# First layer of a two-layer decoder step: where in the input projection the attention's score, transpose and value work stands

## The chip, the core and the metric

The kernel runs on one core of one Trainium2 chip. The metric is the device time of one execution in microseconds. Three runs of the kernel before took 590.7, 591.06 and 591.3 us; the median is 591.06.

Engines are named as in the profile: PE is TensorE (PEld its weight loads), DVE is VectorE, ACT is ScalarE, POOL is GpSimd, SP is the engine that issues most DMAs.

## What is computed

One inference step of two layers over 256 prompt rows (one sequence) and 8 sample rows (each with 256 past positions in paged caches), all with shared weights. The change lies in layer 0, whose mixer is

```python
def moba_gmlp_mixer(x, pos, past_kv, norm_g, w_in, sgu_gain, sgu_w, sgu_b, w_out):
    h = rmsnorm(x, norm_g)
    q, k, v, bu, bv = jnp.split(h @ w_in, ...)
    q, k = rope_partial(q, pos), rope_partial(k, pos)
    a = moba_attention(q, k_all, v_all, pos)          # softmax attention, 8 heads of 64
    bvn = layer_norm(jax.nn.gelu(bv), sgu_gain)
    b_out = spatial_gating(jax.nn.gelu(bu), bvn, sgu_w, sgu_b)   # u * (w @ v + b), chunks of 128
    return x + jnp.concatenate([a, b_out], axis=-1) @ w_out
```

With 256 prompt positions and a block of 256, the prompt's attention is plain causal softmax, and a sample's attention runs over its 256 past positions and its own. After the mixer come a convolution FFN, the second layer (other mixers) and a last norm; the change does not touch them.

## The kernel before

**Projections.** Activations stand transposed (128 partitions by 264 = 256 + 8 columns). Each weight block of 128 x 128 is multiplied in three fp32r matmuls (high x high, low x high, high x low; `mm` in the profile), so one block is 3 mm. Eight blocks make a weight tile: ACT writes its high half (`wh`, L304), DVE the low half (`wl`, L305), into four rotating buffers, three tiles ahead of PE. `run` (L311) goes through the blocks of a phase and calls hooks at given block numbers. Phase `in0` (the input projection of layer 0) has 160 blocks in the order bv, q, k, bu, v; phase `out0` (the output projection) follows and starts with the operand catB.

**Hooks.** `blk(b, f)` places the instructions of `f` behind block b. PE's order is the order in which the program is written (`fixed`, L210); the order of the other engines is set by a scheduler when the kernel is built. It is the same in every execution.

**The work between the blocks.** `s_qk(t)` (L776) multiplies the scores S of one tile of two heads (S_6 and S_7 are those of tile 3) in plain fp32; `s_soft` (L785) takes their maxima with DVE into p (two passes over each S, each followed by a small read of the accumulator into st), exponentiates on ACT and normalizes. `s_tr(t)` (L797) transposes p on PE (`pt`) and copies it to SBUF (`pT`), by ACT for tiles 0 and 1, by DVE for 2 and 3. `sm_score` (L931) multiplies the samples' scores `sc` with the cached keys (32 matmuls and 4 small ones, one PSUM bank); `sm_soft` (L811) is their softmax, `sm_tr` (L830) the transposes. `sample_av` (L519) multiplies them with the cached values (`pv_l`), `sm_out` (L843) transposes that (`po_l`). `v_turn` (L560) transposes the value tiles (`vtp_v`), `s_av` (L801) multiplies the values (`pav`) into catA. `gm_gate` (L910) makes the gate's products `pf`, and DVE and ACT make catB of them. `gm_var` and `gm_norm` are the layer norm of bv (`mu`, `sq`, `bsq`, `ns_sgu`).

**PSUM.** Eight banks: four (`psm`, tag mm) for the projections and some helpers, four (`psa`, tag at, L233) for S, pt, sc, pv_l, po_l, vtp_v and pav. A bank is handed on when its readers are done; the program makes the first matmul of the next owner wait for them.

**Buffers.** A pool of 24 (`up`) holds key and value tiles, p's transposes and other 4 KB tiles by turns.

Of the kernel before, what the change touches and what calls it, by code (L numbers as in the profile page):

```python
# [13 lines left out]
AF = mybir.ActivationFunctionType  # L14
# [192 lines left out]
def tile_decoder_step(ctx: ExitStack, tc: tile.TileContext, a):  # L207
    nc = tc.nc
    v, s, g = nc.vector, nc.scalar, nc.gpsimd
# [25 lines left out]
    def f4(name, shape=(P, 4, T), dt=F32):  # L235
        return up.tile(list(shape), dt, tag="u", name=name)
# [7 lines left out]
    def at(name):  # L244
        return psa.tile([P, 512], F32, tag="at", name=name)
# [217 lines left out]
    def behind(i, j):  # L463

        tc.add_manual_dep(i.ins, j.ins.name, mybir.DependencyInfo(mybir.DependencyClass.NoSync, mybir.DependencyReason.DATA), reason="order")
# [7 lines left out]
    def page_list(cache, name):  # L473

        tiles, todo = [], []

        def load(i):
            if i >= len(regs):
                page_regs(1)
            if i % NPG == 0:  # L480
                tiles.append(f4(f"{name}_{i}", (P, NPG, 512)))
            late(tiles[i // NPG][:, i % NPG, :], cache[bass.ds(regs[i], 1), :, :].rearrange("o p f -> (o p) f"))

        return tiles, [lambda i=i: load(i) for i in range(NS * NPG)]
# [34 lines left out]
    def sample_av(st, pz, vtiles, name):  # L519
        pv = at(f"pv_{name}")  # L520
        for gr in range(2):
            for pg in range(NPG):
                for j in range(4):
                    sq = 4 * gr + j
                    pe.matmul(pv[32 * j:32 * j + 32, :], pz[:, pg, sq, :], vtiles[sq][:, pg, :],
                              start=gr + pg == 0, stop=gr + pg == NPG, skip_group_check=True)
        s.activation(st["msk"], pv, AF.Copy)
# [17 lines left out]
    PZ = con.tile([P, NPG, NS, 32], F32, name="PZ")  # L545
# [5 lines left out]
    def turn(blocks, name, bank=None):  # L551

        ps = [(bank or at)(f"{name}_{r}") for r in range(2)]
        for i, x in enumerate(blocks):
            for r, p in enumerate(ps):
                a0 = r * HF
                pe.transpose(p[:, i * HF:(i + 1) * HF], x[a0:a0 + HF, :], ident[a0:a0 + HF, a0:a0 + HF])
        return ps

    def v_turn(vt, src, ts, name, bank=None, e=None):  # L560
        n = len(ts)
        ps = turn([src[:, t, kb * P:(kb + 1) * P] for kb in range(2) for t in ts], f"vtp_{name}{ts[0]}", bank)
        for r, p in enumerate(ps):
            d, x = vt.rearrange("p b (t r d) -> p b t r d", r=2, d=HF)[:, :, ts[0]:ts[0] + n, r, :], p[:, :2 * n * HF].rearrange("p (b t d) -> p b t d", b=2, t=n)
            v.tensor_copy(d, x) if (e[r] if isinstance(e, tuple) else e) is v else s.activation(d, x, AF.Copy)

    def p_turn(dst, ws, name, pin=False, e=None):
        ps = turn([w[:, i * P:(i + 1) * P] for w in ws for i in range(3)], name)
        for r, p in enumerate(ps):
            d, x = dst.rearrange("p h (i r d) -> p (h i) r d", r=2, d=HF)[:, :, r, :], p[:, :6 * HF].rearrange("p (x d) -> p x d", d=HF)  # L570
            i = v.tensor_copy(d, x) if e is v else s.activation(d, x, AF.Copy)
            if pin:
                tc.keep_in_program_order(i)

    def av(pav, vt, w, h):
        o = pav[64 * (h % 2):64 * (h % 2) + 64, :SEQ]
        pe.matmul(o, vt[:, 0, h * HD:(h + 1) * HD], w[:, :SEQ], start=True, stop=False)
        pe.matmul(o[:, P:], vt[:, 1, h * HD:(h + 1) * HD], w[:, SEQ:], start=False, stop=True)
# [79 lines left out]
    def pick(xg):  # L658
        return lambda m, k: hl(xg, k)
# [107 lines left out]
    vtiles, vload = page_list(a["vp0"], "V0")  # L767
    st0 = {}
# [7 lines left out]
    def s_qk(t):  # L776
        pss, hd = [at(f"S0_{2 * t + i}") for i in range(2)], heads(t)
        for ps, (qh, kh) in zip(pss, hd):
            tc.keep_in_program_order(pe.matmul(ps[:, 0:P], qh[:, 0:P], kh[:, 0:P], start=True, stop=False, skip_group_check=True))
        for ps, (qh, kh) in zip(pss, hd):  # L780
            tc.keep_in_program_order(pe.matmul(ps[:, P:384], qh[:, P:SEQ], kh[:, 0:SEQ], start=False, stop=True, skip_group_check=True))
        for i, ps in enumerate(pss):
            s_soft(2 * t + i, ps)

    def s_soft(h, ps):  # L785
        st = sm.tile([P, 4], F32, tag="st", name=f"st0_{h}")
        pr = pp.tile([P, 384], F32, tag="p", name=f"p0_{h}")
        for i, c in enumerate((slice(0, P), slice(P, 384))):
            v.tensor_tensor_reduce(out=pr[:, c], in0=ps[:, c], in1=maskb0[:, c], scale=-1.0, scalar=-NEG, op0=ALU.add, op1=ALU.min, accum_out=st[:, i:i + 1])
        for i, c in enumerate((slice(0, P), slice(P, 384))):  # L790
            s.activation(pr[:, c], pr[:, c], AF.Exp, bias=st[:, i:i + 1], scale=-1.0, accum_out=st[:, 2 + i:3 + i])
        v.reciprocal(st[:, 2:4], st[:, 2:4])
        v.tensor_scalar(pr[:, 0:P], pr[:, 0:P], st[:, 2:3], None, ALU.mult)
        s.activation(pr[:, P:384], pr[:, P:384], AF.Copy, scale=st[:, 3:4])
        st0["p", h] = pr

    def s_tr(t):  # L797
        pT = st0["pT", t] = f4(f"pT0_{t}", (P, 2, 384))
        p_turn(pT, [st0.pop(("p", 2 * t + i)) for i in range(2)], f"pt0_{t}", e=v if t > 1 else s)

    def s_av(t):  # L801
        w = st0.pop(("pT", t))
# [124 lines left out]
    blk = lambda b, f, *x: hk.at(b / 8 - 1, f, *x)  # L927
# [16 lines left out]
    blk(40, masks)  # L944
    blk(44, gm_first)
    blk(72, sm_q)
    for t, b in enumerate((96, 96, 112, 125)):
        blk(b, s_qk, t)
    for t, b in enumerate((112, 125)):
        blk(b, s_tr, t)  # L950
    blk(96, sgu_load)
    blk(132, sgu_mask)
    blk(90, gm_mean)
    blk(114, gm_var)
    blk(131, sm_score)
    blk(131, sm_soft)
    blk(132, gm_norm)
    blk(140, sm_tr)
    blk(141, gm_gelu)
    blk(143, lambda: nc.sync.dma_start(a["k0"], k4))  # L960
    blk(144, gm_tr)
    blk(144, s_tr, 2)
    blk(144, s_tr, 3)
    blk(152, gm_own)
    for t in range(4):
        blk(152, gm_gate, t)
    blk(159, lambda: sample_av(st0, PZ, vtiles, "l0"))
    run(orders["in0"], pick(xg), in0_evac, hk)
    nc.sync.dma_start(a["v0"], v4)
    hk = Hooks()  # L970
    blk(4, sm_out)
    blk(4, lambda: v_turn(vt, v4, range(4), "v0", e=(s, v)))
    for t in range(4):
        blk(9, s_av, t)
    blk(24, lnexp)
# [13 lines left out]
    vtiles, vload = page_list(a["vp1"], "V1")  # L989
# [64 lines left out]
    def z_tr(t, pin=False):  # L1054
        pT = st1["pT", t] = f4(f"pT1_{t}", (P, 2, 384))
        p_turn(pT, [st1.pop(("w", 2 * t + hh)) for hh in range(2)], f"pt1_{t}", pin)
# [72 lines left out]
    blk = lambda b, f, *x: hk.at(b / 8 - 1, f, *x)  # L1129
# [147 lines left out]
```

## Time and profile before

| | |
|---|---|
| median of 3 runs | 591.06 us |
| the profiled execution: its own time | 591.49 us |
| the profiled execution: its span, first to last instruction | 589.7 us |
| PE busy | 582.5 us, 99% |
| DVE busy | 429.0 us, 73% |
| ACT busy | 338.4 us, 57% |

The profile is of one execution. A timeline row gives start, length, engine, line, operation, output <- input and shape; rows of PE overlap, since matmuls are pipelined and their ends are modelled, so the distance between two starts tells more than a length. "[0.26 <-X]" is idle time of that engine ahead of the row and what ended it.

### The profile page before, as it was taken

The numbers are of one execution on the slowest core, as the hardware profiler recorded it, in microseconds if no ns is written. First come the engines' busy times: TensorE is split into PE (matmuls) and PEld (weight loads), VectorE is DVE, ScalarE is ACT, GpSimd is POOL, SyncE is SP. The second block draws the span as 40 slices with busy tenths as digits, with TensorE's granted clock in tenths as the row PEclk, the third lists the DMA queues.
The fourth block names the chain that finished last, engine by engine and source line by source line (L and its number), as shares of the span: only waits on it lengthen the run. The fifth ranks groups of instructions, "written<-read, shape, count | busy, mean of one in ns | idle before, by whom it ended". The sixth has DMA issues, their size and how long they took to land.

```text
span 589.7 us, 12427 instructions
## 1 busy us (share of the span) xinstructions
PE 582.5 (99%) x4972; PEld 566.3 (96%) x4972; DVE 429.0 (73%) x771; ACT 338.4 (57%) x597; POOL 45.2 (8%) x62
## 2 busy tenths in 40 slices
PE   9999999999999999999999999999999999999995
PEld 7999879999999999999999879999999999999995
DVE  6999876787877877566669675778787777756552
ACT  7849746665655655544454556567565565555431
POOL 1000213200000000011030000120000000002111
PEclk9999999999999999999999999999999999999998
DMA  8899764554545455894557762554554546464501
GB/s 331 327 399 368 265 224 166 189 203 159 211 152 206 161 198 177 298 361 172 197 210 287 262 217 89 180 204 169 189 186 172 202 157 215 150 216 158 201 1 73
DMA packets 27564, 122.42 MB, mean 208 GB/s; under 512 B 3314, under 2 KB 4466, under 8 KB 16114
## 3 DMA queue, kind: packets, MB, share of 16 engines
q1 hardware_dynamic: 27218, 121.28, 57.2%
q8 instruction: 39, 0.64, 0.4%
q10 hardware_dynamic: 288, 0.34, 0.2%
q14 instruction: 19, 0.16, 0.1%
HBM read 117.65 MB, written 3.96 MB: 206 GB/s over the span
## 4 chain that ended last, share of the span: by engine, by line
PE 95%; DMA 1%; DVE 1%; ACT 1%; issue 1%; SPq 0%; POOLq 0%
PE mm L219 89%; PE sc L219 1%; PE pv_l L219 1%; DMA xw<-in_xw 1%; PE pav L219 1%; PE Z L219 1%; PE S L219 1%; PE pt L222 1%; DVE wl L688 0%; PE pf L219 0%; PE pm L219 0%; ACT sqw L670 0%; SPq L370 0%; DVE xg_l L403 0%; DVE sqw L718 0%
## 5 line engine op out<-in xcount | busy, mean ns | idle before, releaser
L304 ACT ACTIVATE wh<-raw 128x1024 fp32r<-128x1024 f32 x177 | 187.4, 1061 | 196.9 <-PE mm L219 183.7
L305 DVE TENSOR_TENSOR wl<-raw,wh 128x1024 fp32r<-128x1024 f32 x177 | 217.4, 1229 | 104.8 <-ACT wh L304 104.2
L219 PE MATMUL mm<-xg_f_h,wh 128*128 128x264 f32 x704 | 199.9, 284 | 0.0
L219 PE MATMUL mm<-xg_f_h,wl 128*128 128x264 f32 x704 | 199.8, 284 | 0.0
L219 PE MATMUL mm<-xg_f_l,wh 128*128 128x264 f32 x704 | 198.6, 282 | 0.0
L219 PEld LDWEIGHTS mm<-xg_f_l,wh 128*128 128x128 f32 x704 | 132.8, 189 | 0.0
L219 PEld LDWEIGHTS mm<-xg_f_h,wh 128*128 128x128 f32 x704 | 132.5, 188 | 0.0
L219 PEld LDWEIGHTS mm<-xg_f_h,wl 128*128 128x128 f32 x704 | 132.4, 188 | 0.0
L219 PE MATMUL mm<-a_h,wl 128*128 128x264 f32 x352 | 100.0, 284 | 0.0
L219 PE MATMUL mm<-a_h,wh 128*128 128x264 f32 x352 | 100.0, 284 | 0.0
L219 PE MATMUL mm<-a_l,wh 128*128 128x264 f32 x352 | 99.7, 284 | 0.0
L219 PEld LDWEIGHTS mm<-a_l,wh 128*128 128x128 f32 x352 | 66.4, 189 | 0.0
L219 PEld LDWEIGHTS mm<-a_h,wh 128*128 128x128 f32 x352 | 66.2, 188 | 0.0
L219 PEld LDWEIGHTS mm<-a_h,wl 128*128 128x128 f32 x352 | 66.2, 188 | 0.0
L219 PE MATMUL mm<-xg_h,wh 128*128 128x264 f32 x160 | 44.4, 293 | 0.2 <-ACT xg_h L402 0.2
L219 PE MATMUL mm<-xg_h,wl 128*128 128x264 f32 x160 | 43.3, 285 | 0.1
L219 PE MATMUL mm<-xg_l,wh 128*128 128x264 f32 x160 | 43.0, 284 | 0.0
L219 PE MATMUL mm<-xg_n_h,wh 128*128 128x264 f32 x128 | 38.0, 297 | 0.0
L219 PE MATMUL mm<-xg_n_h,wl 128*128 128x264 f32 x128 | 36.4, 285 | 0.0
L219 PE MATMUL mm<-xg_n_l,wh 128*128 128x264 f32 x128 | 36.3, 284 | 0.0
L219 PEld LDWEIGHTS mm<-xg_h,wh 128*128 128x128 f32 x160 | 29.2, 189 | 2.3 <-issue 1.2
L219 PEld LDWEIGHTS mm<-xg_h,wl 128*128 128x128 f32 x160 | 29.2, 188 | 0.3 <-DVE wl L688 0.3
(260 smaller groups left out, 842.4 us busy)
## 6 DMA issues: line engine op xcount, KB each, us to landing
raw<-in_w SPq DMA_DIRECT2D x89, 1024.0 KB, 4.8
K<-in_kt SPq DMA_DIRECT2D x32, 256.0 KB, 7.4
V<-in_vp SPq DMA_DIRECT2D x32, 256.0 KB, 5.9
raw<-in_w SPq DMA_DIRECT2D x4, 512.0 KB, 8.7
X<-in_x SPq DMA_DIRECT2D x4, 264.0 KB, 4.6
xw<-in_xw SPq DMA_DIRECT2D x2, 388.0 KB, 4.9
out_y<-yo SPq DMA_DIRECT2D x2, 300.0 KB, 2.3
out_k<-k SPq DMA_DIRECT2D x1, 528.0 KB, 8.9
```

The costliest lines, as they stand in the source:

```text
L219: return self.keep(nc.tensor.matmul(*x, **k))
L222: return self.keep(nc.tensor.transpose(*x, **k))
L304: s.activation(h, src, AF.Copy)
L305: v.tensor_tensor(l, src, h.bitcast(F32), ALU.subtract)
```

## The change

Three hooks of phase `in0` move. The transposes of tile 1 go from block 125 to 128, and the scores of tile 3, which stood ahead of them, from 125 to 128, behind them. The samples' scores and their softmax go from 131 to 128, so that the three stand together. The gate's products go from block 152 to 150. The samples' values go from block 159 of `in0` to block 4 of `out0`, behind the value tiles' transposes, and `sm_out` from block 4 to 9, ahead of `s_av`. Beside that, the copies of pt 2 and 3 go from DVE to ACT, and the exponentials of heads 6 and 7 are ordered behind the last copy of p's transposes on ACT.

```diff
@@ p_turn
             if pin:
                 tc.keep_in_program_order(i)
+        return i
@@ s_soft
-            s.activation(pr[:, c], pr[:, c], AF.Exp, bias=st[:, i:i + 1], scale=-1.0, accum_out=st[:, 2 + i:3 + i])
+            e = s.activation(pr[:, c], pr[:, c], AF.Exp, bias=st[:, i:i + 1], scale=-1.0, accum_out=st[:, 2 + i:3 + i])
+            if h > 5:
+                behind(e, st0["turned"])
@@ s_tr
-        p_turn(pT, [st0.pop(("p", 2 * t + i)) for i in range(2)], f"pt0_{t}", e=v if t > 1 else s)
+        st0["turned"] = p_turn(pT, [st0.pop(("p", 2 * t + i)) for i in range(2)], f"pt0_{t}", e=s)
@@ the hooks of in0 and out0
...
+    blk(128, s_tr, 1)
+    blk(128, s_qk, 3)
...
+    blk(128, sm_score)
+    blk(128, sm_soft)
...
```

On PE, at the samples' scores, the order before was (K are the key tiles, qz the samples' queries; DMAHW, DVE and Activation are the semaphores that an instruction waits for):

```order
L219 MATMUL mm_1104<-xg_h,wh_896 128x264
L219 MATMUL mm_1104<-xg_l,wh_896 128x264
L219 MATMUL mm_1104<-xg_h,wl_897 128x264
L219 MATMUL sc_1114<-K_0_337,qz_l_144 32x256 [waits DMAHW1_49,DMAHW0_49,DVE_49]
L219 MATMUL sc_1114<-K_0_337,qz_l_144 32x256 x3
L219 MATMUL sc_1114<-K_2_406,qz_l_144 32x256 [waits DMAHW4_49,DMAHW3_49]
```

and on the same engine and place it is now:

```order
L222 MATMUL pt_1_1_1061<-CST,p_3_848 128x64
L219 MATMUL S_6_1076<-k_218,q_217 128x128
L219 MATMUL S_7_1077<-k_218,q_217 128x128 [waits Activation_49]
L219 MATMUL S_6_1076<-k_218,q_217 128x256
L219 MATMUL S_7_1077<-k_218,q_217 128x256
L219 MATMUL sc_1100<-K_0_337,qz_l_144 32x256 [waits DMAHW1_49,DMAHW0_49,DVE_49]
L219 MATMUL sc_1100<-K_0_337,qz_l_144 32x256 x3
L219 MATMUL sc_1100<-K_2_406,qz_l_144 32x256 [waits DMAHW4_49,DMAHW3_49]
```

Between S of tile 3 and sc there stood the transposes of tile 1 and 18 mm; now nothing stands there, and sc still waits for a count of DVE.

On DVE, at the passes over S of tile 3, the order before was:

```order
L887 TENSOR_TENSOR bv_220<-bv_220,mu 128x1056
L305 TENSOR_TENSOR wl_1023<-raw_761,wh_1022 128x1024
L789 ISA p_6_1052,st_6_1051<-S_6_1045,maskb_215 128x128
L789 ISA st_6_1051 128x1
L789 ISA p_6_1052,st_6_1051<-S_6_1045,maskb_215 128x256
L789 ISA st_6_1051 128x1
```

and on the same engine and place it is now (wl_1150 is the low half of weight tile 19, bu and bsq belong to the gate's branch):

```order
L890 TENSOR_TENSOR bv_220<-bv_220,mu 128x1056
L305 TENSOR_TENSOR wl_1023<-raw_761,wh_1022 128x1024
L765 TENSOR_TENSOR bu_221<-mm_1026,R_n_373 128x264
L869 TENSOR_TENSOR bsq<-sq_987 128x264
L870 TENSOR_TENSOR bsq<-bsq,sq_987 128x264
L305 TENSOR_TENSOR wl_1150<-raw_761,wh_1149 128x1024
L863 TENSOR_SCALAR tril<-CST 128x128
L871 TENSOR_TENSOR bsq<-bsq,sq_987 128x264
L790 ISA p_6_1083,st_6_1082<-S_6_1076,maskb_215 128x128
L790 ISA st_6_1082 128x1
L790 ISA p_6_1083,st_6_1082<-S_6_1076,maskb_215 128x256
L790 ISA st_6_1082 128x1
```

Six instructions now stand on DVE ahead of the passes over S_6, which before came straight behind the low half of tile 18.

## Rows read from the trace of the kernel before

**Rows 1.** The page: busy PE (us, share, instructions), and the last chain by engine.

```profile
PE 582.5 (99%) x4972; PEld 566.3 (96%) x4972; DVE 429.0 (73%) x771; ACT 338.4 (57%) x597; POOL 45.2 (8%) x62
...
PE 95%; DMA 1%; DVE 1%; ACT 1%; issue 1%; SPq 0%; POOLq 0%
```

**Rows 2.** Waits of PE: us in total, times, longest.

```profile
PE mm L219 <- ACT xg_h L402: 0.2, 1, 0.2
```

**Rows 3.** Timeline of PE, block 125 to the samples' scores: start, length.

```profile
55.57 0.28 PE L219 MATMUL mm<-xg_h,wl 128*128 128x264 f32 x1
55.79 0.93 PE L219 MATMUL S<-k,q 64*128 64x128 f32 x8
56.55 0.54 PE L222 MATMUL pt<-CST,p 64*128 64x64 f32 x12
57.01 0.39 PE L219 MATMUL mm<-xg_h,wh 128*128 128x264 f32 x1
57.24 0.28 PE L219 MATMUL mm<-xg_l,wh 128*128 128x264 f32 x1
...
59.19 0.28 PE L219 MATMUL mm<-xg_h,wl 128*128 128x264 f32 x1
59.41 3.66 PE L219 MATMUL sc<-K,qz_l 128*32 128x256 f32 x64
```

**Rows 4.** Timeline of PE, from behind the gate's products to catB's first.

```profile
74.77 0.37 PE L219 MATMUL mm<-xg_h,wh 128*128 128x264 f32 x1
...
77.48 3.64 PE L219 MATMUL pv_l<-V,PZ 128*32 128x512 f32 x32
81.05 0.39 PE L219 MATMUL mm<-xg_h,wh 128*128 128x264 f32 x1
...
81.52 0.29 PE L219 MATMUL mm<-catB_h,wh 128*128 128x264 f32 x1
```

**Rows 5.** Timeline of DVE at the passes over S_6, and the mask's first step.

```profile
56.37 1.22 DVE L305 TENSOR_TENSOR wl<-raw,wh 128x1024 fp32r<-128x1024 f32 x1
57.51 0.29 DVE L789 CUSTOM_DVE_ANT_0 p<-S,maskb 128x128 f32<-128x128 f32 x1
...
58.06 0.09 DVE L789 DVE_READ_ACCUMULATOR2_ANT st<- 128x1 f32 x1
...
58.27 0.43 DVE L866 TENSOR_TENSOR bsq<-sq 128x264 f32<-128x264 f32 x1
58.62 0.42 DVE L789 CUSTOM_DVE_ANT_0 p<-S,maskb 128x256 f32<-128x256 f32 x1
...
59.38 0.41 DVE L764 TENSOR_TENSOR bu<-mm,R_n 128x264 f32<-128x264 f32 x1
59.71 0.43 DVE L868 TENSOR_TENSOR bsq<-bsq,sq 128x264 f32<-128x264 f32 x1
...
65.01 0.22 DVE L860 TENSOR_SCALAR tril<-CST 128x128 f32<-128x128 f32 x1
```

**Rows 6.** Timeline of ACT: sq, a high half, and the one behind the gelu.

```profile
56.49 1.09 ACT L889 ACTIVATE sq<-bv 128x1056 f32<-128x1056 f32 x1
...
59.61 1.04 ACT L304 ACTIVATE wh<-raw 128x1024 fp32r<-128x1024 f32 x1
...
73.14 1.06 ACT L304 ACTIVATE wh<-raw 128x1024 fp32r<-128x1024 f32 x1 [2.17 <-PE mm L219]
```

**Rows 7.** Timeline of PE: the warm-up at the start, the last matmuls.

```profile
0.78 4.00 PE L219 MATMUL warm<-const-bfloat16-1.0 128*128 128x256 bf16 x18 [0.78 <-PEq L1243]
...
582.76 0.99 PE L219 MATMUL ns_end<-fin,ones 128*128 128x64 f32 x4
```

**Rows 8.** Stretches behind the last matmul: busy by engine, PEclk (granted clock), DMA.

```profile
585.00:585.20 0.20, 0.00 (x0) 0.00 (x0) 0.20 (x1) 0.00 (x0) 0.20 (x1) 0.64 0.00 0
585.20:585.50 0.30, 0.00 (x0) 0.00 (x0) 0.30 (x2) 0.00 (x0) 0.30 (x1) 0.50 0.64 253
```

**Rows 9.** Timeline of DVE: the gate's sums, first and last of the chain.

```profile
73.92 0.75 DVE L914 TENSOR_TENSOR bv<-pf,sguc 128x256 f32<-128x256 f32 x2
...
78.09 1.11 DVE L471 TENSOR_TENSOR catB_l<-bu,catB_h 128x264 fp32r<-128x264 f32 x3
```

More of the change, by code (lines that the diff above doesn't have):

```diff
@@ L946, in tile_decoder_step @@
     blk(72, sm_q)
-    for t, b in enumerate((96, 96, 112, 125)):
+    for t, b in enumerate((96, 96, 112)):
         blk(b, s_qk, t)
-    for t, b in enumerate((112, 125)):
-        blk(b, s_tr, t)
+    blk(112, s_tr, 0)
+    blk(128, s_tr, 1)
+    blk(128, s_qk, 3)
     blk(96, sgu_load)
@@ L954, in tile_decoder_step @@
     blk(114, gm_var)
-    blk(131, sm_score)
-    blk(131, sm_soft)
+    blk(128, sm_score)
+    blk(128, sm_soft)
     blk(132, gm_norm)
@@ L963, in tile_decoder_step @@
     blk(144, s_tr, 3)
-    blk(152, gm_own)
+    blk(150, gm_own)
     for t in range(4):
-        blk(152, gm_gate, t)
-    blk(159, lambda: sample_av(st0, PZ, vtiles, "l0"))
+        blk(150, gm_gate, t)
     run(orders["in0"], pick(xg), in0_evac, hk)
@@ L970, in tile_decoder_step @@
     hk = Hooks()
-    blk(4, sm_out)
     blk(4, lambda: v_turn(vt, v4, range(4), "v0", e=(s, v)))
+    blk(4, lambda: sample_av(st0, PZ, vtiles, "l0"))
+    blk(9, sm_out)
     for t in range(4):
```

## The prediction

> **What bounds the kernel now.** I read the page first: TensorE is busy 99% of the span, and 95% of the chain that ended last is PE [rows 1]. Then the waits of PE: after the start there is one, of 0.2 us [rows 2]. So between 10 and 582 us TensorE never stands still. A cover that is lengthened or an engine that is relieved gains nothing here; time is gained only by PE work that goes away, and whatever makes PE wait is added in full, with nothing later to give it back. The change touches 41 to 89 us, so I read that stretch on PE, DVE and ACT.
>
> The projection's matmuls (mm) follow each other at 0.122 us (57.24 to 59.19 is 16 steps [rows 3]). Between them PE makes visits to plain fp32 work: scores S, transposes pt, samples' scores sc, values pv_l. At each visit the last mm before it takes 0.22 us instead of 0.12 (55.57 to 55.79, 59.19 to 59.41), and the first mm after it 0.23 (57.01 to 57.24) [rows 3]. A visit thus costs about 0.10 + 0.11 = 0.21 us beside its own work.
>
> **The change, part by part.** *Visits.* No matmul is added or removed. Before, S of the last tile with pt of tile 1 is one visit and sc, 18 mm later, another; now pt, S and sc are one. The visit of pv_l, which stood alone from 77.48 to 81.05 [rows 4], joins the value tiles' transposes, and po_l goes over to the visit of pav. That is two visits fewer: 2 x 0.21 = 0.42 us gained. Bounds: if a change of fp32 form inside a visit cost what entering does (0.10 each), 0.2; at most 0.46.
>
> *The wait at sc.* This is the term that decides. The first sc matmul waits for a count of DVE (the order of PE with its waits, above). Followed through the semaphore counts of the built program, it is in both kernels the second read of the maxima of S_6: sc takes over the PSUM bank that S_6 leaves, since the pool of score banks has four. Before, DVE had done that read at 58.06 + 0.09 = 58.15 [rows 5], and sc came at 59.41: 1.26 us to spare, bought by the 18 mm between. Now sc is the next thing PE does after S.
>
> When could PE start sc? S and pt come at block 128 instead of 125, 9 mm later: 55.57 + 9 x 0.122 + 0.22 = 56.89 for pt; pt takes 0.46 (56.55 to 57.01), so S at 57.35; S takes 0.76 (55.79 to 56.55), so sc could start at 58.11 [rows 3].
>
> When has DVE read S_6? Up to and with the wl that starts at 56.37, DVE's order is the same, so it is free at 57.51, as before [rows 5]. Where S_6 came next, there now stand six instructions (the order of DVE, above). bu: 0.33 (59.38 to 59.71), to 57.84. Two of bsq: 0.35 each (58.27 to 58.62), to 58.54. Then wl of tile 19, which waits for its wh on ACT. ACT has sq until 56.49 + 1.09 = 57.58 and then makes that wh in 1.04 [rows 6], to 58.62. wl occupies DVE 1.14 (56.37 to 57.51), to 59.76. tril 0.22, to 59.98; bsq 0.35, to 60.33. Then both passes over S_6 with their reads, 0.64 (57.51 to 58.15), to 60.97 [rows 5]. PE waits 60.97 - 58.11 = 2.86 us. Instructions overlap by about 0.1 us at their ends (wl's 1.22 occupies 1.14), so it may be 0.2 less; and handing over a semaphore takes some hundredths, so I keep 2.86 and call it 2.6 to 3.0.
>
> Queued behind the waiting sc are all of PE's matmuls. ACT's copy of pt 1 reuses the buffer of the first key tile, so it too starts only after the first sc matmuls, and the exponentials of S_6 and S_7 stand behind it on ACT. They end near 64, while PE is in sc until about 64.5, and their transposes come some 6 us later: free.
>
> The Trainium skill, PSUM - Partial Sum Buffer, section Engine vs sequencer instructions, says that the queues of ScalarE, VectorE and GpSimd are strict FIFO; it speaks against putting sc right behind S. The trace agrees: S of the last tile ended at 55.79 + 0.93 = 56.72 [rows 3], and DVE took it up at 57.51, when the wl ahead of it was through [rows 5]. By that rule the wait is the 2.86; with a DVE that took whatever is ready, the price would be that of the third case below.
>
> Sum: 2.86 - 0.42 = +2.4 us. The profiled execution took 591.49 us (its span is 589.7), 0.43 above the median of 591.06; I apply the difference to the median: **593.5 us** if TensorE's clock holds.
>
> *The clock.* S now ends at 57.35 + 0.93 = 58.28, and PE then stands idle for 2.7 us, which happens nowhere in the trace before its end. There, the last matmuls end at 582.76 + 0.99 = 583.75 [rows 7]; the granted clock is 0.64 on average from 585.0 to 585.2 and 0.50 behind that [rows 8]: it fell from 2.4 to 1.2 GHz some 1.3 us after the last matmul, behind 1.7 us of small matmuls with gaps. An idle time of 2.7 us is twice that, so I expect the fall here too. Its price: at the start 18 warm-up matmuls of 256 columns fill 4.00 us [rows 7], 0.22 us each, which is the pace of 1.2 GHz; the 264 columns of mm take 0.12 later. So the way up took about 4.0 us of work. Work at half pace loses half its time: 2.0 us if the clock falls just as sc begins; if it falls 1.3 us into the idle time (59.6) and returns 4.0 later (63.6), 2.6 us of work are at half pace, and 1.3 are lost. Middle, as an estimate: 1.6 us. That gives 593.5 + 1.6 = **595.1 us**, my forecast. Bounds of this term: 0 and 2.0.
>
> *Without cost.* The copies of pt 2 and 3 go from DVE to ACT, four copies of 384 columns; ACT idles there for 2.17 us, waiting for PE to free a weight buffer [rows 6], and the copies' first reader, pav, stands behind the start of the output projection. The gate's products come 6 mm earlier; their operands on DVE and GpSimd are ready, as the mask is made earlier too. pv_l moved later needs nothing that isn't there.
>
> **The rivals.** *The clock holds*: 593.5. For it: full activity on both sides of the gap, where the fall at the end had sparse work ahead. The Trainium skill, TensorE: Matmul & The Clock Gate, section Why this matters for your kernels, has a rule by which a gap like this one does not yet bring the clock down; by it this case is the time. The fall at the end of this trace speaks against it.
>
> *DVE is at S_6 in time* (not slower than before). If DVE took up S_6 when S ends, at 58.28, its 0.64 us would end at 58.92, the wait would be 0.8 and the time 591.06 + 0.8 - 0.42 = 591.4; with no wait at all, 590.6. It decides from a wait of 1.6 us: below that the sum stays within 0.2% of before, which is about what a measurement of this kernel can tell from no change. That needs DVE at S_6 by 59.07, ahead of wl. Against it: wl stands ahead in the built order and cannot end before 59.7. For it: only an error of mine in which count sc waits for.
>
> *A second wait, at the first matmuls of the output projection.* pv_l no longer stands between the gate and catB's first use. Before, catB was needed 81.52 - 74.77 = 6.75 us after the gate's products, three mm behind 81.05; now that is 6.75 - 3.78 (the visit of pv_l with its 0.21) + 0.73 (6 mm) = 3.7 [rows 4], and 1.2 more for the fourth pair: 4.9. DVE's chain ran from 73.92 to 78.09 + 1.11 = 79.20 [rows 9], 5.28 us with one wl in it; from 0.85 before the end of the products that leaves 4.43, and 4.77 with the value evacuation that now stands in it. 0.1 to 0.5 us are to spare. If they fail, up to one wl, so 0.5 us on top: 595.6.
>
> **How the numbers follow.** Wait with the fall of the clock: 0.50 (595.1, from 594.6 to 595.6 by the bounds). Wait, clock holds: 0.29 (593.5, from 593.1 to 593.8). With the second wait on top: 0.06. DVE in time: 0.13, nearly all within 0.2%. Something faster that I do not see: 0.02. The first three are all slower by over 0.2% (592.24): 0.85; same 0.13; faster 0.02. The range goes from 592.9 to 595.8, which takes in the first three cases but their tails, and leaves out the fourth.
>
> **What would show it.** The waits of PE name sc behind DVE with 2.6 to 3.0 us, and the row of sc on PE starts near 60.9 with S before it near 57.4. On DVE the passes over S_6 start near 60.3, behind wl. If the clock fell, the granted clock is 0.50 in a stretch of some 2 to 4 us near 60 to 64, and sc takes longer than its 3.6 us. PE shows no other wait; catB's first matmuls follow the projection's at 0.12. The forecast is wrong if sc starts within 1.6 us of S's end, or if the stall is there and the total is below 592.2, which would mean that PE has slack somewhere that I have not seen.

## The result and the profile after

The changed kernel takes 596.59 us (median of 6 executions, 595.58 to 598.43), the kernel before 591.25 us beside it (6 executions, 590.7 to 591.41): a ratio of 1.0092, 95% interval 1.0082 to 1.0102. It is slower, as forecast, by 5.3 us where 4.0 were forecast, and 0.8 us over the upper end of the range.

| | before | after |
|---|---|---|
| median | 591.25 us | 596.59 us |
| the profiled execution: its own time | 591.49 us | 596.42 us |
| its span | 589.7 us | 594.6 us |
| first ns_sgu on PE | 63.50 us | 67.80 us (4.30 later) |
| first pav on PE | 86.01 us | 90.31 us (4.30 later) |

The page of the profile after, the rows that answer to [rows 1] (busy PE, chain by engine), and its row of the granted clock in 40 slices:

```profile
PE 584.7 (98%) x4972; PEld 568.1 (96%) x4972; DVE 428.0 (72%) x767; ACT 339.8 (57%) x601; POOL 44.4 (7%) x62
PEclk9999899999999999999999999999999999999998
PE 93%; DMA 3%; DVE 2%; ACT 1%; issue 1%; SPq 0%; POOLq 0%; ACTq 0%; DVEq 0%
```

Chain and busy shares hardly move; of 4.9 us the page itself shows an 8 in the clock's fifth slice, 59 to 74 us. The waits of PE after (us in total, times, longest) answer to [rows 2]:

```profile
PE sc L219 <- DVE st L790: 2.7, 1, 2.7
PE warm L219 <- PEq L1247: 0.8, 1, 0.8
PE mm L219 <- DVE bv L765: 0.4, 1, 0.4
```

There is the one new wait, under the name it was forecast with. The wait of 0.4 us stands at 24 us, ahead of the change, where the kernel before had 0.2 us for ACT; by 54 us the starts of PE's matmuls in the two profiles are the same again within 0.1 us. The timeline of PE after answers to [rows 3] (start, length):

```profile
56.66 0.28 PE L219 MATMUL mm<-xg_h,wl 128*128 128x264 f32 x1
56.87 0.59 PE L222 MATMUL pt<-CST,p 64*128 64x64 f32 x12
57.29 0.88 PE L219 MATMUL S<-k,q 64*128 64x128 f32 x8
60.91 5.35 PE L219 MATMUL sc<-K,qz_l 128*32 128x256 f32 x64 [2.74 <-DVE st L790]
66.08 0.22 PE L219 MATMUL sc<-ones,own 128*32 128x1 f32 x8
66.22 0.39 PE L219 MATMUL mm<-xg_h,wh 128*128 128x264 f32 x1
```

The reader sees two losses in two rows: 2.74 us ahead of sc, and sc itself. From its start to the next mm it takes 66.22 - 60.91 = 5.31 us; before it took 63.03 - 59.41 = 3.62 us, by the start of sc in [rows 3] and this row of the kernel before:

```profile
63.03 0.39 PE L219 MATMUL mm<-xg_h,wh 128*128 128x264 f32 x1
```

That is 1.69 us more. The stretches of the kernel after (busy us by engine, then PEclk, the granted clock) say why:

```profile
58.00:60.00 2.00, 0.17 (x2) 0.00 (x0) 1.97 (x5) 0.47 (x1) 0.00 (x0) 1.00 0.51 126
60.00:61.00 1.00, 0.09 (x4) 0.09 (x8) 1.00 (x8) 0.42 (x1) 0.16 (x1) 1.00 1.04 394
61.00:62.00 1.00, 1.00 (x16) 0.59 (x20) 0.74 (x5) 0.31 (x1) 0.77 (x2) 0.66 0.62 176
62.00:64.00 2.00, 2.00 (x28) 0.96 (x24) 0.45 (x2) 2.00 (x9) 1.10 (x1) 0.50 0.92 299
64.00:65.00 1.00, 1.00 (x17) 0.53 (x13) 0.45 (x2) 1.00 (x4) 0.00 (x0) 0.63 0.96 373
```

From 61.3 to 64.7 us (0.68, 2.00 and 0.74 us of the last three rows) the clock was 1.2 GHz, and all of that stretch lies within sc. What kept DVE is in its own timeline, which answers to [rows 5]:

```profile
57.45 0.43 DVE L765 TENSOR_TENSOR bu<-mm,R_n 128x264 f32<-128x264 f32 x1
57.79 0.42 DVE L869 TENSOR_TENSOR bsq<-sq 128x264 f32<-128x264 f32 x1
58.25 0.43 DVE L870 TENSOR_TENSOR bsq<-bsq,sq 128x264 f32<-128x264 f32 x1
58.60 1.22 DVE L305 TENSOR_TENSOR wl<-raw,wh 128x1024 fp32r<-128x1024 f32 x1
59.74 0.22 DVE L863 TENSOR_SCALAR tril<-CST 128x128 f32<-128x128 f32 x1
59.87 0.43 DVE L871 TENSOR_TENSOR bsq<-bsq,sq 128x264 f32<-128x264 f32 x1
60.22 0.28 DVE L790 CUSTOM_DVE_ANT_0 p<-S,maskb 128x128 f32<-128x128 f32 x1
...
60.77 0.09 DVE L790 DVE_READ_ACCUMULATOR2_ANT st<- 128x1 f32 x1
```

The six instructions of the built order stand ahead of S_6 without a gap; the second read of its maxima ends at 60.86, and sc starts 0.05 later.

So by the first ns_sgu 4.30 us are lost, and by pav the same 4.30. The span is longer by 594.6 - 589.7 = 4.9 us. The last 0.6 us were lost later, where the change moves nothing. Stretches of 100 us in the first layer's FFN, of the kernel before and then of the one after, show it in the count of matmuls:

```profile
130.00:230.00 100.00, 100.00 (x832) 100.00 (x831) 76.61 (x138) 58.36 (x106) 0.00 (x0) 1.00 0.52 183
```

```profile
130.00:230.00 100.00, 100.00 (x828) 100.00 (x827) 76.68 (x141) 57.15 (x104) 0.00 (x0) 1.00 0.52 185
```

PE is busy all the time at 2.4 GHz in both, waits for nothing, and gets four matmuls fewer done. Start by start, mm follow each other at 120.55 ns before and at 121.1 ns after, from 115 to 241 us; in the second layer's FFN (410 to 510 us) both have 832. The same matmul comes 4.31 us later than before at 112 us, 4.89 us later at 244 us and 4.90 us later from there to the end.

### The profile page after: what moved, and what is told of

Same layout as the page of the kernel before. It is cut to its first block, busy times and chain, and to the rows that moved or that the text cites. A ratio compares the mean times of both kernels' runs of the same rounds, so it can differ in the third digit from the quotient of the medians.

```text
span 594.6 us, 12434 instructions
## 1 busy us (share of the span) xinstructions
PE 584.7 (98%) x4972; PEld 568.1 (96%) x4972; DVE 428.0 (72%) x767; ACT 339.8 (57%) x601; POOL 44.4 (7%) x62
## 4 chain that ended last, share of the span: by engine, by line
PE 93%; DMA 3%; DVE 2%; ACT 1%; issue 1%; SPq 0%; POOLq 0%; ACTq 0%; DVEq 0%
PE mm L219 87%; DMA raw<-in_w 2%; PE sc L219 2%; PE pv_l L219 1%; DMA xw<-in_xw 1%; PE pav L219 1%; DVE wl L305 1%; PE Z L219 1%; PE pt L222 0%; PE S L219 0%; PE pf L219 0%; PE pm L219 0%; ACT p L792 0%; SPq L370 0%; DVE bv L890 0%
## 5 line engine op out<-in xcount | busy, mean ns | idle before, releaser
L219 PEld LDWEIGHTS mm<-xg_l,wh 128*128 128x128 f32 x160 | 29.6, 192 | 0.0
```

Of the source, the lines that this page charges most:

```text
L219: return self.keep(nc.tensor.matmul(*x, **k))
```

## Experiments

Three questions: are wait and clock the loss, and do they hang together (e1 to e4, e7, e8)? Does the rest of the change matter (e5, e6)? What makes the step longer behind 115 us (e5, e6, e9 to e15)? The ratio is to the kernel before on the same chip.

| run | median, us | ratio (95%) |
|---|---|---|
| e1_apart | 591.55 | 1.0005 (0.9997 to 1.0014) |
| e2_visit_only | 595.45 | 1.0061 (1.0045 to 1.0077) |
| e3_fill | 595.90 | 1.0077 (1.0064 to 1.0090) |
| e4_sc_ahead | 592.53 | 1.0021 (1.0013 to 1.0030) |
| e5_values_undone | 591.58 | 1.0002 (0.9993 to 1.0011) |
| e6_gate_undone | 597.94 | 1.0117 (1.0101 to 1.0134) |
| e7_fill4 | 595.30 | 1.0074 (1.0060 to 1.0088) |
| e8_sc_9mm | 593.54 | 1.0047 (1.0027 to 1.0067) |
| e9_place | 596.65 | 1.0093 (1.0079 to 1.0107) |
| e10_place_half | 597.09 (one execution) | |
| e11_place_as_e5 | 596.28 | 1.0093 (1.0076 to 1.0110) |

**e1: the merged visit undone**, with the order of the exponentials that goes with it.

```diff
...
-    for t, b in enumerate((96, 96, 112)):
+    for t, b in enumerate((96, 96, 112, 125)):
         blk(b, s_qk, t)
-    blk(112, s_tr, 0)
-    blk(128, s_tr, 1)
-    blk(128, s_qk, 3)
+    for t, b in enumerate((112, 125)):
+        blk(b, s_tr, t)
...
-    blk(128, sm_score)
-    blk(128, sm_soft)
+    blk(131, sm_score)
+    blk(131, sm_soft)
```

> The changed kernel with only the merged visit undone: the last score tile, turned probabilities and samples' scores stand at blocks 125, 125 and 131 as in the kernel before; the copies of the turned probabilities on ScalarE, the gate's products at block 150 and the samples' values beside the value tiles' transposes stay. Theory A (the whole loss is the wait of the samples' scores for VectorE plus the fall of the clock behind it; the rest of the change is worth about nothing): no wait of PE at sc, granted clock 1.00 through 55 to 70 us, pav at 86.0 us within 0.1, time 591.2 us (590.9 to 591.5). Theory B (part of the 5.3 us comes from the other edits, since wait and clock make only 4.3 of it by the trace): about 0.6 us of it stays, 591.9 us (591.7 to 592.2).

591.55 us, 1.0005: wait and low clock are gone with the visit. PE's waits name no sc, the granted clock is 1.00 throughout 58 to 66 us, and sc takes its old time:

```profile
58.69 3.66 PE L219 MATMUL sc<-K,qz_l 128*32 128x256 f32 x64
```

By the medians (591.37 us beside it) the rest of the change cannot be told from nothing, and 591.55 lies between the ranges of the two theories. The trace decides for theory B's 0.6 us: it has the longer step (828 matmuls in 130 to 230 us), and from the first pav to PE's last matmul it takes 498.01 us, where the kernel before takes 497.42. Its span is no longer (589.6 us, before 589.7) because PE came to S of the last tile at 55.07 us in this profile and at 55.79 in the one before, ahead of the first hook that differs.

**e2: only the merged visit** (the kernel before with the hooks of the merged visit, and the order of the exponentials that goes with it).

> The kernel before with only the merged visit of the change (pt, last score tile and samples' scores at block 128, and the order of ScalarE that goes with it); the copies of the third and fourth turned tile, the gate and the samples' values as before. Theory A: the whole loss is here: sc waits 2.7 us for VectorE, the granted clock falls to 0.50 for about 3.4 us, sc takes 5.3 us, and the time is that of the changed kernel, 596.5 us (596.0 to 597.0). Theory B (the other edits cost 0.6): 595.9 us or less, with the offset to the kernel before at pav still 4.3 us.

595.45 us; the trace repeats wait and clock:

```profile
60.62 5.35 PE L219 MATMUL sc<-K,qz_l 128*32 128x256 f32 x64 [2.78 <-DVE st L790]
```

From S to ns_sgu it takes 67.51 - 56.97 = 10.54 us, the changed kernel 67.80 - 57.29 = 10.51. What is missing to the changed kernel is 1.1 us at the medians. 0.6 of it is the step: its FFN runs at the short pace (832 matmuls). The rest fits a clock that did not fall every time: of its six executions two took 593.55 and 594.06 us with a mean granted clock of 0.997, four 595.4 to 596.63 us with 0.994 or 0.995.

**e3 and e7: the wait filled with work** (seven, then four more rounds of S_7's own matmuls behind the first).

```diff
             tc.keep_in_program_order(pe.matmul(ps[:, P:384], qh[:, P:SEQ], kh[:, 0:SEQ], start=False, stop=True, skip_group_check=True))
+        for i in range(4 if t == 3 else 0):
+            tc.keep_in_program_order(pe.matmul(ps[:, 0:P], qh[:, 0:P], kh[:, 0:P], start=True, stop=False, skip_group_check=True))
+            tc.keep_in_program_order(pe.matmul(ps[:, P:384], qh[:, P:SEQ], kh[:, 0:SEQ], start=False, stop=True, skip_group_check=True))
```

> The changed kernel with extra work of TensorE in the place of the wait: the two matmuls of the last head's scores (S_7) are done eight times instead of once, the same products each time, ahead of the samples' scores. VectorE reads S_6 as late as in the changed kernel, so sc starts at the same time (60.9 us, a wait of 0.0 to 0.3 us is left), but TensorE has not stood still. Theory A (the idle time brings the clock down, and that costs 1.7 us): the granted clock stays at 1.00, sc takes 3.5 to 3.6 us, ns_sgu comes at 66.1 us, and the time is 1.7 us less than that of the changed kernel, 594.9 us (594.5 to 595.2). Rival C (the slow sc has another cause than the idle time, its place behind S or its data): sc takes 5.2 us again and the time is 596.6 us.

> As e3, with the two matmuls of S_7 done five times instead of eight, since one repetition took 0.65 us there: 2.6 us of extra work in the wait of 2.7. Theory A: sc starts 3.6 us after S as in the changed kernel, waits 0.3 us at most, granted clock 1.00, sc takes 3.53 instead of 5.2 us, and the time is 1.7 us under the changed kernel's: 594.9 us (594.4 to 595.4). Rival C (clock or sc are slow for another reason): 596.6 us.

In e3 the work was too long (S 5.46 us), so that what the clock gave back was spent again: 595.9 us. The expected time failed by the size of the filling. e7 has the right amount. Its timeline and clock:

```profile
56.82 3.49 PE L219 MATMUL S<-k,q 64*128 64x128 f32 x24
60.56 3.66 PE L219 MATMUL sc<-K,qz_l 128*32 128x256 f32 x64 [0.25 <-DVE st L793]
64.04 0.22 PE L219 MATMUL sc<-ones,own 128*32 128x1 f32 x8
64.19 0.39 PE L219 MATMUL mm<-xg_h,wh 128*128 128x264 f32 x1
```

```profile
60.00:62.00 2.00, 1.75 (x30) 0.92 (x32) 1.27 (x9) 1.14 (x3) 1.51 (x2) 1.00 0.44 110
62.00:64.00 2.00, 2.00 (x44) 1.18 (x39) 0.54 (x3) 2.00 (x10) 0.58 (x1) 1.00 0.98 369
```

sc still starts 60.56 - 56.82 = 3.74 us behind S, as in the changed kernel (3.62), but PE has worked meanwhile, the clock stays at 2.4 GHz, and sc takes 3.63 us. From S to ns_sgu it is 65.75 - 56.82 = 8.93 us, 1.58 less than in the changed kernel. The median moved by less, 1.3 us, in the direction and within the spread of both.

One profile would not show that the idle time is the cause, since the clock held once without any filling (e11, below). The mean granted clocks of all executions do: of the 43 executions of e1, e3, e4, e5 and e7, which leave PE at most 0.25 us of wait there, none is below 0.996; of the 28 of the changed kernel, e2, e8 to e11 and e13, which leave it 2 us or more in every profile, 17 are. So the idle time brings the clock down, in most executions and not in all. The price is the same in every profile with the low clock at sc but e9's: sc takes 5.31 us to the next mm in the changed kernel, e2, e8, e10 and e13, and 3.63 in e1, e7 and e11.

**e4: the samples' scores ahead of S** (the same visit in the order pt, sc, S; ACT's copies of pt ahead of the squares' sum).

```diff
...
-    blk(128, s_qk, 3)
     blk(96, sgu_load)
...
     blk(128, sm_score)
+    blk(128, gm_cut)
+    blk(128, s_qk, 3)
     blk(128, sm_soft)
```

> The changed kernel with the three steps still in one visit, in another order: turned probabilities, samples' scores, last score tile. The samples' scores then take a bank that was read long before; the last score tile (S_7) takes the bank of the first turned half, whose copy ScalarE makes meanwhile (it is put ahead of the gate's squares there). Theory A (only the wait for the bank and the clock cost something, and one visit less is worth 0.1 to 0.3 us): no wait of PE or one of up to 0.3 us at S, granted clock 1.00, time 591.0 us (590.7 to 591.4). Rival D (three kinds of work in one visit cost as such): sc or S is longer than before by itself, time over 592.

There is no wait in the visit, and the clock is 1.00 there, as theory A says, but the time is 592.53, not 591.0 us. The gain of a saved visit did not come: ns_sgu lies 63.73 - 57.02 = 6.71 us behind the visit's start, and 63.50 - 55.79 = 7.71 before with 9 mm (1.09 us) more in between, so the merged visit took 0.1 us longer, not less. That is rival D's sign, in small: sc took 3.59 us to the start of S behind it, where it took 3.47 to its own small matmuls before (59.41 to 62.88), and S 0.85 us to the next start, where it took 0.76. And the gate's norm (L903) came to DVE only at 68.03 us, so that the transposes which read it went matmul by matmul, 1.44 us for 16 where e1 has 0.71:

```profile
68.03 1.70 DVE L903 SCALAR_TENSOR_TENSOR bv<-bv,VEC,R_sgu 128x264 f32<-128x264 f32 x4
```

```profile
68.88 1.44 PE L222 MATMUL vtp_sgu<-CST,bv 64*128 64x64 f32 x16
```

The wait had moved on to the next reader of the same engine, without a name in the list of waits: from ns_sgu to pav e4 takes 23.14 us, e1 22.47. With the longer step (828 matmuls) that makes 0.1 + 0.7 + 0.6 = 1.4 us, against 1.2 by the medians.

**e8: sc 9 mm later** (`sm_score` and `sm_soft` at block 131 in the changed kernel, nothing else).

> The changed kernel with the samples' scores 9 matmuls of the projection later (block 131 instead of 128), a visit of their own again. They could start 1.4 us later, while VectorE reads S_6 when it did: a wait of 1.3 to 1.5 us is left. If the clock falls behind a wait of that size too: sc takes over 4 us, time 595 us. If it holds (the fall at the end of the kernel before came 1.3 us after the last matmul, so by that row it is on the edge; I take 0.6 that it holds): sc takes 3.5 us and the time is 2.74 - 1.4 = 1.35 us for the wait, 0.1 for the visit and 0.6 for the slower steps behind 120 us: 593.3 us.

```profile
56.67 0.87 PE L219 MATMUL S<-k,q 64*128 64x128 f32 x8
...
58.54 0.28 PE L219 MATMUL mm<-xg_h,wl 128*128 128x264 f32 x1
60.86 5.35 PE L219 MATMUL sc<-K,qz_l 128*32 128x256 f32 x64 [2.04 <-DVE st L790]
```

2.04 us are left instead of 1.35, since DVE and ACT were further behind PE in this execution: the read of S_6's maxima ended 4.14 us behind the start of S, in the changed kernel's profile 3.57 (60.86 - 57.29). The clock fell here (PEclk 0.50 from 62 to 64 us). But of five executions of the same program two took 595.24 and 596.1 us with a mean granted clock of 0.995, and three 593.2 to 593.54 us with 0.997 to 0.999. By these means the clock fell in two executions of one program and held in three, about 2 us apart; only one of the five, a fall, was profiled.

**e5 and e6: the rest of the change, in two halves.** Both start from e1. e5 undoes the samples' values, e6 the gate:

```diff
 e5
-    blk(4, lambda: sample_av(st0, PZ, vtiles, "l0"))
-    blk(9, sm_out)
+    blk(159, lambda: sample_av(st0, PZ, vtiles, "l0"))
+    blk(4, sm_out)
 e6
-    blk(150, gm_own)
+    blk(152, gm_own)
     for t in range(4):
-        blk(150, gm_gate, t)
+        blk(152, gm_gate, t)
```

> Only two of the change's edits: the copies of the turned probabilities on ScalarE and the gate's products at block 150. The scores and the samples' values stand as in the kernel before. In this build the projections take their PSUM banks in the order of the changed kernel, and the feed-forward operand tiles of the first layer lie in places of their own (two of the four as in the changed kernel). Theory P (the slower step comes from where these operand tiles lie in SBUF, above all the second half's two): steps of 120.55 ns from 120 to 240 us, time as before, 591.3 us. Theory Q (it comes from the order of the PSUM banks): 121.1 ns there, 0.6 us more, 591.9 us.

> Only two of the change's edits: the copies of the turned probabilities on ScalarE and the samples' values beside the value tiles' transposes. The scores and the gate stand as in the kernel before. In this build the projections take their PSUM banks in the order of the kernel before, while the first layer's feed-forward operand tiles lie otherwise than before. Theory P (placement of the operand tiles): may be either, 121.1 ns if the second half's high part beside its neighbour is what counts. Theory Q (order of the banks): 120.55 ns from 120 to 240 us, time as before, 591.3 us.

e5 is the kernel before in time (591.58, 1.0002). e6 is the slowest of all. Its waits of PE:

```profile
PE mm L219 <- DVE catB_l L471: 1.0, 1, 1.0
...
PE mm L219 <- ACT catB_h L468: 0.3, 1, 0.3
```

```profile
78.97 0.39 PE L219 MATMUL mm<-catB_h,wh 128*128 128x264 f32 x1 [0.26 <-ACT catB_h L468]
80.37 0.39 PE L219 MATMUL mm<-catB_l,wh 128*128 128x264 f32 x1 [1.00 <-DVE catB_l L471]
```

This is the second wait of the prediction's rival, at catB's first matmuls, and behind it the clock is 0.50 from 82 to 84 us. Without the 6 mm by which the gate comes earlier, moving the values costs 1.3 us of waits and a fall of the clock, together 3.6 us from ns_sgu to pav (26.09 us, in e5 22.48), and that in the shortest of its four executions (595.39 us; the others took 597.58 to 598.96). With them the changed kernel shows a single stumble of 0.09 us at this place: 82.74 - 82.53 = 0.21 where mm follow at 0.12.

```profile
82.53 0.37 PE L219 MATMUL mm<-catB_l,wh 128*128 128x264 f32 x1
82.74 0.28 PE L219 MATMUL mm<-catB_h,wl 128*128 128x264 f32 x1
```

For the longer step: e5 takes its projections' PSUM banks in the order of the changed kernel and has 832 matmuls in 130 to 230 us, e6 takes them in the order before and has 828. Theory Q falls.

**e9 to e11: only the place of the FFN's operand tiles** (a read on GpSimd keeps earlier tiles allocated; e9 holds two, e10 one, e11 three).

```diff
+    xg0 = xg
     xg, nrm, evac = residual(vec("f0"), "f0")
     run(orders["out0"], pick([catA, catB]), evac, hk)
+    hold = sm.tile([P, 1], F32, tag="hold", name="hold", bufs=1)
+    for x in (xg0[1][0], xg0[1][1]):
+        g.tensor_tensor(hold, x[:, 0, 0:1].bitcast(F32), xg[1][1][:, 0, 0:1].bitcast(F32), ALU.add)
```

> The changed kernel, with two one-column reads on GpSimd that keep the second operand tiles of the first projections allocated a little longer, so that the feed-forward operand's second half (xg_f01, high and low part) is put into two other places of the same pool. Nothing else of TensorE's work or its order changes. Theory P (place of these tiles): matmuls step at 120.55 ns from 120 to 240 us instead of 121.1, and the time is 0.6 us under the changed kernel's, with the wait and the fall of the clock as they were: 596.0 us. Rival (something else that e5 and e6 share with the two groups): 121.1 ns, 596.6 us.

> As e9, but only the low part of the second half lies in another place than in the changed kernel; the high part keeps its own. Theory P with both parts needed: 121.1 ns a step from 120 to 240 us; if it is enough to move one of the two: 120.55 ns. No forecast which; it narrows the place down.

> The changed kernel, with three one-column reads on GpSimd that keep three earlier tiles allocated a little longer; by that all four tiles of the first layer's feed-forward operand (two halves, high and low part) lie at the addresses that they have in e5, where the step was 120.55 ns. Order, waits and clock as in the changed kernel. Theory P (these four addresses decide): 120.55 ns a step from 120 to 240 us, 0.6 us under the changed kernel, 596.0 us. Rival (the addresses of these four are not it, it is something else that the move of the samples' values changes): 121.1 ns, 596.6 us. After e9 and e10 I give each a half.

All three have 828 matmuls in 130 to 230 us, e11 too, with the four tiles where they lie in e5 (e10 took 597.09 us with a wait of 3.5 us and a clock that fell). Theory P falls as well. Beside that they show how far wait and clock swing. In e9 the wait was 2.81 us and the clock low for twice as long:

```profile
58.00:60.00 2.00, 0.00 (x0) 0.00 (x0) 2.00 (x7) 0.33 (x1) 0.00 (x0) 0.85 0.69 197
60.00:62.00 2.00, 1.76 (x20) 0.84 (x24) 1.06 (x7) 0.70 (x3) 1.60 (x2) 0.50 0.95 305
62.00:64.00 2.00, 2.00 (x24) 0.94 (x20) 0.45 (x2) 2.00 (x10) 0.41 (x1) 0.50 0.95 351
64.00:66.00 2.00, 2.00 (x24) 0.98 (x20) 0.45 (x2) 0.80 (x3) 0.00 (x0) 0.50 1.03 380
66.00:68.00 2.00, 2.00 (x33) 1.57 (x22) 0.43 (x1) 0.56 (x2) 0.00 (x0) 0.94 0.78 298
```

sc took 66.80 - 60.24 = 6.56 us there, 2.94 over its old time. In e11 the wait was 3.46 us, longer than in any profile but e10's, and the clock held:

```profile
61.81 3.66 PE L219 MATMUL sc<-K,qz_l 128*32 128x256 f32 x64 [3.46 <-DVE st L790]
```

```profile
62.00:64.00 2.00, 2.00 (x41) 1.17 (x37) 0.65 (x3) 1.48 (x5) 1.77 (x2) 1.00 0.99 336
```

**e12 to e15: four kernels profiled a second time**, unchanged: the kernel before, the changed one, e1 and e5 (591.1, 596.72, 591.36 and 590.87 us, one execution each).

> The kernel before, profiled once more. If the step from 120 to 240 us belongs to the kernel: 120.55 ns again, as in its first trace. If it changes from execution to execution: either, and then at least one of the four profiles of this set differs from its first.

> The changed kernel, profiled once more. If the step belongs to the kernel: 121.1 ns from 120 to 240 us; if it is chance, either. The wait at sc between 2.7 and 3.5 us, and the granted clock at 0.50 behind it in most executions, not in all (e8 and e11 had executions in which it held).

> e1 once more (the changed kernel with the merged visit undone). If the step belongs to the kernel: 121.1 ns from 120 to 240 us, as in e1; if it is chance, either.

> e5 once more (only the copies on ScalarE and the gate at block 150). If the step belongs to the kernel: 120.55 ns from 120 to 240 us, as in e5; if it is chance, either.

| | first profile, matmuls in 130 to 230 us | second |
|---|---|---|
| before (e12) | 832 | 832 |
| after (e13) | 828 | 828 |
| e1 (e14) | 828 | 828 |
| e5 (e15) | 832 | 832 |

The step belongs to the kernel. e1 and e5 differ by the place of the samples' values alone, and all kernels with the moved values (after, e1, e3, e4, e6 to e11, e13, e14) have 828, all others (before, e2, e5, e12, e15) 832. From the first pav to PE's last matmul the first twelve take 498.01 to 498.02 us, the other five 497.42. So the longer step comes with that move, and costs 0.60 us. How it reaches into the FFN 30 us later was not found: PE's instructions there are the same in number and order, with as many waits, and bank order and operand place are out. In e13 the wait was 2.8 us and the clock fell, as in the first profile of the changed kernel.

The medians do not show the 0.60 us: e1 and e5 differ by 0.03 us, with eleven executions each. In both profiles of e1 PE started the last matmul ahead of S at 54.86 us, 0.1 to 0.7 us earlier than in those of e5 and of the kernel before (54.99 to 55.57). Whether e1 wins that time in every execution was not tested.

No version here beats the kernel before; e1 and e5 cannot be told from it.

## Why the prediction was right, and where not

**The wait at sc: right.** Forecast 2.86 us (2.6 to 3.0), with sc free to start at 58.11, 0.76 behind the start of S, and DVE through with S_6 at 60.97. Counted in the same way it was 60.91 - (57.29 + 0.76) = 2.86; the 2.74 of the page counts from the modelled end of S, 58.17. DVE's read ended at 60.86; bu came at 57.45 for 57.51, the second wl at 58.60 for 58.62, the passes at 60.22 for 60.33. The order of six instructions on DVE, each with a duration from [rows 5] and [rows 6], gave the end of the read within 0.11 us. That the wait itself agrees to the hundredth is luck: PE was 0.06 us early too, and 0.05 passed between the read and sc. The sequence of DVE that was built is what PE's wait is read from, by the rule on strict queues that the prediction took from the Trainium skill (PSUM - Partial Sum Buffer, section Engine vs sequencer instructions); the trace agrees, with wl at 58.60 ahead of an S that had been there since 58.2. Not seen was that this wait swings: 2.0 us were left in e8 where 1.35 were expected, and e11 had 3.46.

**The clock: right in the profiled execution.** Forecast 1.6 us (1.3 to 2.0); measured 1.69, with PEclk 0.50. It fell later than forecast, 0.4 us after sc had begun rather than in the idle time, and returned later, which leaves the price nearly the same. That case stood at 0.50 against 0.29 for a clock that holds, and by the mean clocks both happen in one and the same program (e2, e8, e11). A loss of 2.94 us, as in e9, lay outside the bound of 2.0. The 4.0 us that the prediction took over from the warm-up were read from its pace alone: the PEclk of the kernel before is 1.00 there (0.8 to 4.4 us). The prediction's lesson from the end of the kernel before [rows 8], that a gap of such a size brings the clock down, held in most executions; the rule against it (the Trainium skill, TensorE: Matmul & The Clock Gate, section Why this matters for your kernels) did not in the profiled execution, where 2.74 us of wait were followed by 0.50, and in e8 2.04 us were enough, while in e11 3.46 us were not.

**The visits: mis-sized.** Forecast 0.42 us gained, bounds 0.2 to 0.46. To ns_sgu the loss is 4.30, wait and clock make 2.86 + 1.69 = 4.55, so the first merged visit gained 0.25, where 0.21 were forecast (0.13, if the wait is counted as the page does). From ns_sgu to pav nothing more was gained (22.51 us before and after, 22.47 in e1, 22.48 in e5), where 0.21 were forecast. One way in and one way out were saved there too, but 0.09 us went in the stumble at catB, and work inside the visit got longer. po_l took 83.38 - 83.08 = 0.30 us to the next start, and takes 90.31 - 89.91 = 0.40, in the kernel before and then in the one after:

```profile
83.08 0.46 PE L222 MATMUL po_l<-CST,msk 64*128 64x64 f32 x8
83.38 0.67 PE L222 MATMUL vtp_v<-CST,v 64*128 64x64 f32 x16
```

```profile
89.91 0.47 PE L222 MATMUL po_l<-CST,msk 64*128 64x64 f32 x8
90.31 0.88 PE L219 MATMUL pav<-pT,vt 128*64 128x256 f32 x8
```

vtp_v, now with pv_l behind it, takes 0.64 for 0.60. So it was wrong to take the inside of a visit as free: leaving one kind of work for another costs there too, and e4's visit, with one transition more inside, even grew by 0.1 us. Worth 0.2 us.

**Without cost.** The gate and the values were taken as free with 0.1 to 0.5 us to spare. Measured is 0.09 us of stumbling at catB, so nothing was to spare; e6 shows the 3.6 us that stood behind that edge. The copies on ACT cost nothing that a trace shows.

**The step that failed: nothing behind 89 us.** "The change touches 41 to 89 us, so I read that stretch": by that the prediction put the time of everything behind it at no change, without a reason. The runs show 0.60 us there, the largest miss in the sum: 4 matmuls in 832, 0.5% of the stretch from 115 to 241 us, in every profile with the moved values and in none without. No row of the kernel before could have given its size: it is not a wait, and the work there is the same. Its cause stays open.

Together: 2.86 + 1.69 - 0.25 + 0.6 = 4.9 us, which is the difference of the spans (4.9) and of the profiled executions (596.42 - 591.49 = 4.93). Forecast were 2.86 + 1.6 - 0.42 = 4.04. Of the 0.9 between them 0.6 are the step, 0.2 the visits and 0.1 the clock. The median is 596.59 - 595.1 = 1.5 us over the forecast: these 0.9, 0.2 because the kernel before took 591.25 beside it for 591.06, and 0.4 because the medians differ by 5.34 us (4.8 to 6.0 by the interval), more than the profiled pair. No trace shows the last part. The executions of the changed kernel spread over 2.9 us where those of the kernel before spread over 0.7, which fits a wait and a low clock that swing from one execution to the next: the longest, 598.43 us, had a mean granted clock of 0.991, the profiled one 0.994, and 0.003 of 596 us is 1.8 of the 2.0 us between them. The range was too narrow since each term of it was one execution's, and its end at 595.8 was below the sum of its own upper bounds, 591.06 + 3.0 - 0.2 + 2.0 = 595.86, before the second wait; the bound of the clock should have been open upward.

## What to carry to other kernels

Where PE never waits, read a merge of its steps from the queue of the engine that frees the next buffer: the merge saved 0.25 us here at best, and it takes away the distance that this engine had. Put the instruction order of that engine together with durations from a trace, and the wait in a like execution comes out to a tenth of a microsecond. Count a stall of PE with a second price, the clock, that may come in one execution and not in the next (here behind 2.04 us in e8, behind 0.26 and 1.00 us in e6), and allow for both in the range. Compare two profiles from the last instruction that they share: the last matmul ahead of the change starts anywhere from 54.77 to 55.84 us in the 17 profiles of this case. And follow the comparison to the end of the kernel, not only to the end of the edit.

## What the runs showed of the hardware

- The granted clock fell behind a wait of 2.04 us (e8's profile) and behind waits of 0.26 and 1.00 us (e6's), and held behind 3.46 (e11's); in e8 it fell in two of five executions by their mean clock. It was low for 3.4 us in the changed kernel and 6.8 in e9, at 1.69 and 2.94 us of lost time.
- Work in the wait keeps the clock: e7's PE was busy for all but 0.25 us of it, PEclk stayed 1.00, and the mean clock of its five executions was 0.997 to 0.999.
- A change from one kind of matmul to another costs time inside a visit too: po_l took 0.40 us to the start of pav and 0.30 to that of vtp_v, S 0.85 to the small matmuls of sc and 0.76 to pt.
- A stretch of 126 us in which PE is never idle and the clock is 2.4 GHz can run at 120.55 or 121.1 ns a matmul, by an edit 30 us earlier that leaves the stretch's own instructions as they were; it made 0.60 us in each of twelve profiles and nothing in the five without the edit. The cause is open.
